# Batched matrix product on one core: outputs of two batches in one tile, stores of 6 KB rows, and another order of the rows of x in its loads

## The chip, the cores and the metric

The kernel runs on one core of one Trainium2 chip. The metric is the time of one execution in microseconds, as the device measures it. Before the change the median of nine runs is 136.33 us (lowest 136.18, highest 136.52).

## The reference

```python
batch, dim_i, dim_j, dim_k = 32, 256, 512, 384
x: (batch, dim_i, dim_j) float32
y: (batch, dim_j, dim_k) float32

def reference(x, y):
    return np.einsum('bij,bjk->bik', x, y).astype(np.float32)
```

There are 32 independent products of a 256 x 512 matrix by a 512 x 384 matrix. x is 16.8 MB, y 25.2 MB and the output 12.6 MB; each has to be moved once, 54.5 MB in all.

## The kernel before

The index j, over which the sum runs, has to lie in the partitions for the products. y comes so from memory (`load`, L69): partition q gets the four rows j = 4q to 4q + 3 of a batch, 6 KB in one run. x has j as its last index and has to be transposed on TensorE. It is loaded for four batches at once (Q = 4, L63), 2 MB, each partition taking 16 KB in one run: 32 partitions a batch, 8 rows of i in each.

`transpose(q)` (L71) makes 32 transposes of 128 x 128 for four batches, four to a PSUM bank `t_ps`. Each bank is then cast to fp16 into `xt_sb` by one copy, on DVE (L92) and ACT (L94) in turn; the copy writes with a step of four fp16 elements, so that a batch's 128 columns of i come to lie side by side. `round_y(b)` (L97) casts y of one batch to fp16 in four pieces, two on ACT (L102) and two on DVE (L104). `multiply(b)` (L106) makes eight products, each with 128 columns of x^T as weights and 384 columns of y streaming, into two banks `o_ps`, one for each half e of i. `collect(b)` (L124) copies the two banks to `o_sb`, one on ACT (L128) and one on DVE (L130). `store(b)` (L133) writes `o_sb` to memory, 3 KB in one run from each partition.

The order is written out by hand and kept (`keep`). The loop goes over the steps s = 0 to 33, and in each step issues, in this order: the loads of batch s + 6 (with x of four batches ahead of y where s + 6 is a multiple of four), the copies of batch s - 2, the products of batch s - 1, at every fourth step the transposes of four batches, the rounding of batch s, and the store of batch s - 2. Loads of the first six batches stand ahead of the loop.

All 72 DMAs, loads and stores, are issued by SP in this order, from one queue. In the compiled program they use eight completion counters in turn, and each DMA waits until the DMA eight places before it has finished; a store also waits for the copies on ACT and DVE, and a load of x for the transposes that free its buffer. Buffers: three for x, ten for y, four for rounded y, two for x^T, ten for `o_sb`; in PSUM four banks for `t_ps` and four for `o_ps`.

Of the kernel before, what the change touches and what calls it, by code (L numbers as in the profile page):

```python
# [1 line left out]

# [5 lines left out]


MM_DT = mybir.dt.float16  # L10
F32 = mybir.dt.float32
P = 128


Q = 4

LAG = 8

ON_ACT = ()


@with_exitstack
def kernel(
    ctx: ExitStack,
    tc: tile.TileContext,
    x: bass.AP,
    y: bass.AP,
    out: bass.AP,
):
    nc = tc.nc  # L30

    B, I, J = x.shape
    _, _, K = y.shape

    NI = I // P
    NJ = J // P


    R = Q * NI
    PQ = P // Q  # L40

    const_pool = ctx.enter_context(tc.tile_pool(name="const", bufs=1))
    x_pool = ctx.enter_context(tc.tile_pool(name="x_pool", bufs=3))
    y_pool = ctx.enter_context(tc.tile_pool(name="y_pool", bufs=10))
    yr_pool = ctx.enter_context(tc.tile_pool(name="yr_pool", bufs=4))
    xt_pool = ctx.enter_context(tc.tile_pool(name="xt_pool", bufs=2))
    o_pool = ctx.enter_context(tc.tile_pool(name="o_pool", bufs=10))
    tpsum_pool = ctx.enter_context(tc.tile_pool(name="tpsum", bufs=4, space=bass.MemoryType.PSUM))
    opsum_pool = ctx.enter_context(tc.tile_pool(name="opsum", bufs=4, space=bass.MemoryType.PSUM))


    keep = tc.keep_in_program_order

    identity = const_pool.tile([P, P], F32)
    make_identity(nc, identity)

    x_of, y_of, yr_of, xt_of, ps_of, o_of = {}, {}, {}, {}, {}, {}

    def load(b):
        if b % Q == 0:  # L60
            x_of[b // Q] = x_pool.tile([P, R, J], F32, name="x_sb")
            keep(
                nc.sync.dma_start(  # L63
                    out=x_of[b // Q],
                    in_=x[b : b + Q].rearrange("g (p r) j -> (g p) r j", r=R),
                )
            )
        y_of[b] = y_pool.tile([P, NJ, K], F32, name="y_sb")
        keep(nc.sync.dma_start(out=y_of[b], in_=y[b].rearrange("(q t) k -> q t k", q=P)))  # L69

    def transpose(q):  # L71

        x_sb = x_of.pop(q)
        xt_of[q] = xt_pool.tile([P, Q, NJ, NI, PQ, Q], MM_DT, name="xt_sb")
        n = 0
        for t in range(NJ):
            for e in range(NI):  # L80
                t_ps = tpsum_pool.tile([P, Q, Q, PQ], F32, name="t_ps")
                for h in range(Q):
                    keep(
                        nc.tensor.transpose(  # L84
                            t_ps[:, h].rearrange("c g p -> c (g p)"),
                            x_sb[:, h * NI + e, t::NJ],
                            identity,
                        )
                    )
                dst = xt_of[q][:, :, t, e].rearrange("c g p h -> c h g p")  # L90
                if n % 2 == 0:
                    keep(nc.vector.tensor_copy(dst, t_ps))  # L92
                else:
                    keep(nc.scalar.copy(dst, t_ps))  # L94
                n += 1

    def round_y(b):  # L97
        y_sb = y_of.pop(b)
        yr_of[b] = yr_pool.tile([P, NJ, K], MM_DT, name="y_r")
        for t in range(NJ):  # L100
            if t % 2 == 0:
                keep(nc.scalar.copy(yr_of[b][:, t], y_sb[:, t]))  # L102
            else:
                keep(nc.vector.tensor_copy(yr_of[b][:, t], y_sb[:, t]))  # L104

    def multiply(b):  # L106
        xt_sb, y_r = xt_of[b // Q][:, b % Q], yr_of.pop(b)
        ps_of[b] = [
            opsum_pool.tile([P, K], F32, name=f"o_ps_{e}", tag="o_ps")
            for e in range(NI)  # L110
        ]
        for t in range(NJ):
            for e in range(NI):
                keep(
                    nc.tensor.matmul(  # L115
                        ps_of[b][e],
                        xt_sb[:, t, e].rearrange("c p h -> c (p h)"),
                        y_r[:, t],
                        start=(t == 0),
                        stop=(t == NJ - 1),  # L120
                    )
                )

    def collect(b):  # L124
        o_of[b] = o_pool.tile([P, NI, K], F32, name="o_sb")
        for e in range(NI):
            if e % 2 == 0:
                keep(nc.scalar.copy(o_of[b][:, e], ps_of[b][e]))  # L128
            else:
                keep(nc.vector.tensor_copy(o_of[b][:, e], ps_of[b][e]))  # L130
        del ps_of[b]

    def store(b):  # L133
        eng = nc.scalar if b in ON_ACT else nc.sync
        keep(eng.dma_start(out=out[b].rearrange("(m e) k -> m e k", m=P), in_=o_of.pop(b)))  # L135


    ahead = LAG - 2
    for b in range(ahead):
        load(b)  # L140
    for s in range(B + 2):
        if s + ahead < B:
            load(s + ahead)
        if s >= 2:
            collect(s - 2)
        if 1 <= s <= B:
            multiply(s - 1)
        if s < B and s % Q == 0:
            transpose(s // Q)
        if s < B:  # L150
            round_y(s)
        if s >= 2:
            store(s - 2)


# [1 line left out]
_INS = ['x', 'y']  # L157
_OUTS = [((32, 256, 384), 'float32')]


# [23 lines left out]
```

## Time and profile before

| what | value |
|---|---|
| median of nine runs | 136.33 us |
| profiled execution, its own time | 136.32 us |
| its span, first to last instruction | 134.5 us |
| granted TensorE clock, mean | 0.904 |
| moved in the span | 54.62 MB, mean 406 GB/s |
| read from HBM / written to HBM | 41.94 MB / 12.58 MB |
| DMA packets | 10375, of which 1152 under 512 B |
| loads of y: number, size, issue to landing | 32, 768 KB, 15.1 us (median) |
| loads of x | 8, 2048 KB, 14.1 us |
| stores | 32, 384 KB, 14.1 us |
| first DMA issued | at 0.74 us |

The page divides the span into 40 slices and gives for each engine, and for the 16 DMA engines together, the busy share in tenths. A packet is one run of data as one DMA engine moves it: one 16 KB row of x, one 6 KB row of y, one 3 KB row of the output. The packets under 512 B carry no data; there are 16 for each of the 72 DMAs. "Issue to landing" is long because many DMAs stand in the queue at a time, so it tells of the queue, not of one transfer. The time of the profiled execution lies 1.8 us above its span.

### The profile page before, as it was taken

Reading aid. Unit: us, or ns where it says so; the run is one execution under the profiler, and the core shown is the slowest. Engines: PE = TensorE matmul, PEld = TensorE weight load, DVE = VectorE, ACT = ScalarE, POOL = GpSimd, SP = SyncE. Lnnn points to the kernel's source line nnn. Section 1 sums busy time; section 2 is a strip of 40 time slices with the busy share of each in tenths; the row PEclk is TensorE's granted clock in tenths of the full one; section 3 lists DMA queues with packets and bytes.
Section 4 is the critical chain, followed back from the end, with each engine's and each line's share of the span. In section 5 each row is a group of like instructions: output and inputs, shape, how many; then the busy total and the mean of one; then the engine's idle time right before and its main releaser. Section 6 shows DMA issues by size and latency. Waiting matters only on the chain.

```text
span 134.5 us, 1539 instructions
## 1 busy us (share of the span) xinstructions
PE 89.5 (67%) x512; PEld 65.5 (49%) x512; DVE 73.1 (54%) x128; ACT 79.8 (59%) x129; POOL 0.7 (1%) x6
## 2 busy tenths in 40 slices
PE   0039499949994938869195895949259492785900
PEld 0049346934693518735194454825159260783500
DVE  0007925893489614966079361977018870487610
ACT  3006965697579902996059860998009990289710
POOL 2000000000000000000000000000000000000000
PEclk9999959995999995999959589999968999689997
DMA  5999999999999999999999999999999999999992
GB/s 117 424 393 422 441 418 416 418 452 395 409 417 452 421 407 418 427 439 432 391 429 415 444 427 413 421 412 448 418 410 421 417 469 398 416 423 412 412 414 108
DMA packets 10375, 54.62 MB, mean 406 GB/s; under 512 B 1152, under 2 KB 1152, under 8 KB 9344
## 3 DMA queue, kind: packets, MB, share of 16 engines
q1 hardware_dynamic: 10368, 54.53, 98.1%
q8 instruction: 4, 0.07, 0.2%
q14 instruction: 3, 0.02, 0.0%
HBM read 41.94 MB, written 12.58 MB: 405 GB/s over the span
## 4 chain that ended last, share of the span: by engine, by line
DMA 90%; PE 1%; issue 1%; ACT 1%; SPq 1%; DVE 1%; DVEq 0%
DMA y_sb<-in_y_dram 47%; DMA out_dram<-o_sb 22%; DMA x_sb<-in_x_dram 21%; PE t_ps L84 1%; ACT y_r L102 1%; SPq L69 1%; DVE o_sb L130 0%; SPq L63 0%; DVE y_r L104 0%; ACT o_sb L128 0%; SPq L135 0%; DVEq L130 0%
## 5 line engine op out<-in xcount | busy, mean ns | idle before, releaser
L94 ACT CAST xt_sb<-t_ps 128x512 f16<-128x512 f32 x32 | 39.4, 1366 | 41.6 <-PE t_ps L84 41.5
L92 DVE CAST xt_sb<-t_ps 128x512 f16<-128x512 f32 x32 | 39.5, 1329 | 38.0 <-PE t_ps L84 38.0
L115 PE MATMUL o_ps<-y_r,xt_sb 128*128 128x384 f16 x256 | 48.1, 351 | 15.3 <-ACT y_r L102 15.3
L84 PE MATMUL t_ps<-identity,x_sb 128*128 128x128 f32 x256 | 41.8, 331 | 23.1 <-DMA x_sb<-in_x_dram 23.1
L84 PEld LDWEIGHTS t_ps<-identity,x_sb 128*128 128x128 f32 x256 | 39.5, 215 | 26.3 <-issue 24.9
L115 PEld LDWEIGHTS <-xt_sb 128*128 128x128 f16 x256 | 26.8, 105 | 35.7 <-issue 22.0
L102 ACT CAST y_r<-y_sb 128x384 f16<-128x384 f32 x64 | 30.1, 526 | 0.6 <-DMA y_sb<-in_y_dram 0.6
L130 DVE COPY o_sb<-o_ps 128x384 f32<-128x384 f32 x32 | 17.8, 555 | 17.0 <-PE o_ps L115 16.2
L104 DVE CAST y_r<-y_sb 128x384 f16<-128x384 f32 x64 | 19.8, 352 | 0.4 <-DMA y_sb<-in_y_dram 0.4
L128 ACT COPY o_sb<-o_ps 128x384 f32<-128x384 f32 x32 | 15.4, 483 | 5.6 <-PE o_ps L115 5.6
L94 ACT ACT_TABLE_LOAD x1 | 1.3, 1283 | 0.7 <-PEq L168 0.7
masks.py:199 POOL TENSOR_SCALAR_AFFINE_SELECT identity<-identity 128x128 f32<-128x128 f32 x1 | 0.3, 294 | 0.1
masks.py:197 POOL MEMSET identity<- 128x128 f32 x1 | 0.2, 205 | 0.3 <-POOLq L168 0.3
L168 POOL MEMSET const-bfloat16-1.0<- 128x1 bf16 x1 | 0.1, 102 | 0.0
L168 POOL MEMSET const-uint8-127<- 128x1 uint8 x1 | 0.1, 102 | 0.0
L168 POOL MEMSET const-float32-0.0<- 128x1 f32 x1 | 0.1, 99 | 0.2 <-issue 0.2
L168 POOL MEMSET const-float32-1.0<- 128x1 f32 x1 | 0.1, 99 | 0.0
## 6 DMA issues: line engine op xcount, KB each, us to landing
y_sb<-in_y_dram SPq DMA_DIRECT2D x32, 768.0 KB, 15.1
x_sb<-in_x_dram SPq DMA_DIRECT2D x8, 2048.0 KB, 14.1
out_dram<-o_sb SPq DMA_DIRECT2D x32, 384.0 KB, 14.1
```

The source lines that it names most:

```text
L69: keep(nc.sync.dma_start(out=y_of[b], in_=y[b].rearrange("(q t) k -> q t k", q=P)))
L84: nc.tensor.transpose(t_ps[:, h].rearrange("c g p -> c (g p)"), x_sb[:, h * NI + e, t::NJ], identity,)
L92: keep(nc.vector.tensor_copy(dst, t_ps))
L94: keep(nc.scalar.copy(dst, t_ps))
L102: keep(nc.scalar.copy(yr_of[b][:, t], y_sb[:, t]))
L104: keep(nc.vector.tensor_copy(yr_of[b][:, t], y_sb[:, t]))
L115: nc.tensor.matmul(ps_of[b][e], xt_sb[:, t, e].rearrange("c p h -> c (p h)"), y_r[:, t], start=(t == 0), stop=(t == NJ - 1),)
L128: keep(nc.scalar.copy(o_of[b][:, e], ps_of[b][e]))
L130: keep(nc.vector.tensor_copy(o_of[b][:, e], ps_of[b][e]))
L168: nc = _bacc.Bacc("TRN2", target_bir_lowering=False, num_devices=1)
```

## The change

G = 2 batches form a unit. For a unit, each product takes only 64 columns of x^T, and the two batches of the unit write into the lower and the upper 64 partitions of the same bank `o_ps`: a unit has four banks (e = 0 to 3) with eight products each. `collect` copies four full banks of a unit, and `store` writes two batches in one DMA, 6 KB in one run from each partition. y is still loaded batch by batch, 6 KB rows, two DMAs into one tile. The two halves of the transposes of four batches stand in two successive steps. Loads of x are issued one unit of y earlier. The loop runs over 16 units in 18 steps, with loads two units (four batches) ahead; buffers are halved in number where a buffer now holds two batches.

The load of x takes the same 128 pieces of 16 KB of four batches, but piece s = 16 v + w (v = 0 to 7, w = 0 to 15) goes to partition 8 w + v instead of partition s. The source of the DMA is written as 16 x 8 x 4096 elements (w, v, element), the destination as 128 partitions. The transposes put the columns back in order as they write to PSUM: the output is written with a step of 16 elements in runs of 8.

```diff
 Q = 4
-LAG = 8
+G = 2
+W = 16
+LAG = 4
...
-    NI = I // P
+    M = P // G
+    NE = I // M
     NJ = J // P
-    R = Q * NI
     PQ = P // Q
+    R = I // PQ
+    H = R // NE
+    U = B // G
...
-    y_pool = ctx.enter_context(tc.tile_pool(name="y_pool", bufs=10))
-    yr_pool = ctx.enter_context(tc.tile_pool(name="yr_pool", bufs=4))
+    y_pool = ctx.enter_context(tc.tile_pool(name="y_pool", bufs=5))
+    yr_pool = ctx.enter_context(tc.tile_pool(name="yr_pool", bufs=2))
...
-    o_pool = ctx.enter_context(tc.tile_pool(name="o_pool", bufs=10))
+    o_pool = ctx.enter_context(tc.tile_pool(name="o_pool", bufs=5))
...
-                    in_=x[b : b + Q].rearrange("g (p r) j -> (g p) r j", r=R),
+    def load_x(q):
+        x_of[q] = x_pool.tile([P, R, J], F32, name="x_sb")
+        keep(
+            nc.sync.dma_start(
+                out=x_of[q],
+                in_=x[q * Q : (q + 1) * Q]
+                .rearrange("g (p r) j -> (g p) (r j)", r=R)
+                .rearrange("(v w) s -> w v s", w=W),
+            )
+        )
+    def load(u):
+        if u == 0:
+            load_x(0)
+        if (u + 1) * G % Q == 0 and u + 1 < U:
+            load_x((u + 1) * G // Q)
+        y_of[u] = y_pool.tile([P, G, NJ, K], F32, name="y_sb")
+        for g in range(G):
+            keep(
+                nc.sync.dma_start(
+                    out=y_of[u][:, g],
+                    in_=y[u * G + g].rearrange("(q t) k -> q t k", q=P),
+                )
+            )
+    def transpose(q, half):
+        x_sb = x_of[q]
+        if half == 0:
+            xt_of[q] = xt_pool.tile([P, NJ, NE, Q * PQ, H], MM_DT, name="xt_sb")
+        n = 0
+        for t in range(half * NJ // 2, (half + 1) * NJ // 2):
+            for e in range(0, NE, 2):
+                t_ps = tpsum_pool.tile([P, 2, H, Q * PQ], F32, name="t_ps")
+                for f in range(2):
+                    for h in range(H):
+                        keep(
+                            nc.tensor.transpose(
+                                t_ps[:, f, h].rearrange("c (v w) -> c w v", w=W), x_sb[:, h * NE + e + f, t::NJ], identity
+                            )
+                        )
+                dst = xt_of[q][:, t, e : e + 2].rearrange("c f p h -> c f h p")
...
+    def multiply(u):
+        xt_sb, y_r = xt_of[u * G // Q], yr_of.pop(u)
+        ps_of[u] = []
+        for e in range(NE):
+            o_ps = opsum_pool.tile([P, K], F32, name="o_ps")
+            ps_of[u].append(o_ps)
+            for t in range(NJ):
+                for g in range(G):
+                    a = (u * G + g) % Q
+                    keep(
+                        nc.tensor.matmul(
+                            o_ps[g * M : (g + 1) * M],
+                            xt_sb[:, t, e, a * PQ : (a + 1) * PQ].rearrange("c p h -> c (p h)"),
+                            y_r[:, g, t],
+                            start=(t == 0),
+                            stop=(t == NJ - 1),
+                        )
+                    )
...
+    def store(u):
+        keep(
+            nc.sync.dma_start(
+                out=out[u * G : (u + 1) * G].rearrange("g (m e) k -> (g m) e k", e=NE),
+                in_=o_of.pop(u),
+            )
+        )
     ahead = LAG - 2
-    for b in range(ahead):
-        load(b)
-    for s in range(B + 2):
-        if s + ahead < B:
+    for u in range(ahead):
+        load(u)
+    for s in range(U + 2):
+        if s + ahead < U:
             load(s + ahead)
+        if s == 0:
+            transpose(0, 0)
+            transpose(0, 1)
         if s >= 2:
             collect(s - 2)
-        if 1 <= s <= B:
+        if 1 <= s <= U:
             multiply(s - 1)
-        if s < B and s % Q == 0:
-            transpose(s // Q)
-        if s < B:
+        if s < U:
             round_y(s)
+        for half in range(2):
+            q = (s + 1 - half) * G // Q
+            if (s + 1 - half) * G % Q == 0 and 0 < q < B // Q:
+                transpose(q, half)
         if s >= 2:
             store(s - 2)
```

`round_y` and `collect` keep their copies, with an index for the batch or the bank added.

## The prediction

> **What bounds the kernel now.** I read the page first: the slices of part 2, the queue of part 3 and the chain of part 4.
>
> ```profile
> PE 89.5 (67%) x512; PEld 65.5 (49%) x512; DVE 73.1 (54%) x128; ACT 79.8 (59%) x129; POOL 0.7 (1%) x6
> ...
> DMA  5999999999999999999999999999999999999992
> ...
> q1 hardware_dynamic: 10368, 54.53, 98.1%
> ...
> DMA 90%; PE 1%; issue 1%; ACT 1%; SPq 1%; DVE 1%; DVEq 0%
> ```
>
> The reader is to see that the 16 DMA engines are never idle between the first slice and the last, that their packets fill 98.1% of the span (0.981 x 134.5 = 131.9 us), and that no other engine passes 67%. So the kernel is bound by what its transfers cost, row by row, and a change counts as far as it changes that sum, or opens a hole in it.
>
> Next I asked what one row costs, in three stretches in which one kind of transfer runs alone: 4 to 7 us (x), 9 to 12 us (y) and 125 to 130 us (stores).
>
> ```profile
> DMA packets 76, 1.25 MB, mean 415 GB/s; under 512 B 0, under 2 KB 0, under 8 KB 0
> q1 hardware_dynamic: 76, 1.25, 97.7%
> ```
>
> ```profile
> DMA packets 240, 1.28 MB, mean 426 GB/s; under 512 B 32, under 2 KB 32, under 8 KB 240
> q1 hardware_dynamic: 240, 1.28, 102.0%
> ```
>
> ```profile
> DMA packets 757, 2.07 MB, mean 414 GB/s; under 512 B 84, under 2 KB 84, under 8 KB 757
> q1 hardware_dynamic: 757, 2.07, 103.0%
> ```
>
> Share times 16 engines times length, over the rows (packets under 512 B left out: they carry no data): x 0.977 x 48 / 76 = 0.617 us for a 16 KB row; y 1.02 x 48 / 208 = 0.2354 us for 6 KB; stores 1.03 x 80 / 673 = 0.1224 us for 3 KB. Check: 1024 x 0.617 + 4096 x 0.2354 + 4096 x 0.1224 = 2097 us over 16 engines = 131.1 us, against 131.9.
>
> Last the compute side, from the groups and from stretches of pure work at full clock (16 transposes, then 32 products):
>
> ```profile
> L94 ACT CAST xt_sb<-t_ps 128x512 f16<-128x512 f32 x32 | 39.4, 1366 | 41.6 <-PE t_ps L84 41.5
> L92 DVE CAST xt_sb<-t_ps 128x512 f16<-128x512 f32 x32 | 39.5, 1329 | 38.0 <-PE t_ps L84 38.0
> ...
> L102 ACT CAST y_r<-y_sb 128x384 f16<-128x384 f32 x64 | 30.1, 526 | 0.6 <-DMA y_sb<-in_y_dram 0.6
> L130 DVE COPY o_sb<-o_ps 128x384 f32<-128x384 f32 x32 | 17.8, 555 | 17.0 <-PE o_ps L115 16.2
> ```
>
> ```profile
> core 0: us, PE busy (x) PEld busy (x) DVE busy (x) ACT busy (x) POOL busy (x), PEclk, DMA share, GB/s
> 83.02:84.90 1.88, 1.88 (x16) 1.88 (x16) 1.19 (x2) 0.71 (x1) 0.00 (x0) 1.00 1.03 425
> 58.45:63.60 5.15, 5.15 (x32) 3.02 (x31) 3.12 (x9) 4.41 (x11) 0.00 (x0) 1.00 1.05 439
> ```
>
> The weight loads (3.02 us) lie inside the 5.15 us of the products: 161 ns a product. Transposes are 118 ns each at full clock and, in the stretch 51 to 53 us at clock 0.50, ten in 2.00 us. Compute waits for data most of the time; this is the cover that the change draws on.
>
> [...] a 16 KB row in 0.617 us is 26.6 GB/s on each engine, all 16 at once. [...]
>
> **The change part by part.**
>
> *Stores.* 32 stores of 3 KB rows become 16 of 6 KB rows. 4096 x 0.1224 = 501 us of engine time goes; 2048 rows of 6 KB come, priced like a y row, 2048 x 0.2354 = 482 us. (501 - 482) / 16 = 1.2 us less. That a 6 KB write costs what a 6 KB read does is bounded by the 3 KB rows: at worst twice 0.1224, which is no gain. I take -1.2.
>
> *Loads of x.* The bytes and the rows are the same. [...] a row takes about twice 0.617 us. Sum: 1024 x 0.617 / 16 = 39.5 us becomes 78; the fixed part of a row and of the slow first rows isn't doubled, so I take +38. Bounds: the least is -1, a gain at the start (between 1.8 and 8.8 us the queue moved 364 GB/s, at 420 that is 0.9 us shorter; elsewhere an x row is as quick per byte as a y row, 0.0386 us per KB against 0.0392, so there is nothing to gain in reading); the most is +40. I take the upper, since the engines have no slack: what a row costs more is paid in full.
>
> *Products.* 256 of 128 columns become 512 of 64 columns, in pairs that fill two halves of one bank. For two batches (a unit, 16 in all) that is 32 products. Overlapped in pairs: 16 x 161 ns = 2.6 us; one after another: 5.15 us. I take overlap[...]. Per unit the compute now forms one chain, because the four banks of a unit are all there are: products 2.6, 16 transposes 1.9, the last cast 1.3, the first copy 0.56 = 6.4 us, against (131.9 - 1.2) / 16 = 8.2 us of transfers, or 10.5 with slow x. Hidden; not hidden when the products don't overlap (8.9 us).
>
> *Transposes and casts.* The transposes now write PSUM in runs of single elements 64 B apart; bound 0 to 1.9 us a unit (twice as slow); I take 0. Casts keep count and size (64 of 512), with a destination step of 4 B instead of 8 B: between 1.35 us and half of it. Both lie under the transfers.
>
> *Order, buffers, waits.* SP issues load(s+2) ahead of store(s-2), both in units, so four loads of a unit stand between y(u)'s landing and store(u), as far ahead as before. A store waiting for its copies holds the loads behind it on SP; with up to eight DMAs in flight (each waits for the eighth before it) some 16 us of transfers are queued by then, against a collect about 14 us after its y landed (8.2 of the next unit's transfers, 2.0 of rounding, 2.6 of two casts, 1.0 of copies). One bank is now read by a copy that serves two batches: same copies, 64. No hole.
>
> *The end.* Stores 11 to 15 are left when the last y row has landed: four of them, 4 x 128 x 0.2354 / 16 = 7.5 us, lie ahead of the last. Its own chain: rounding 1, products 2.6 to 5.2[...], copy 0.6, issue and start about 1.5 = 5.7 to 8.3 us. 0 to 0.8 exposed; I take 0.3. The old end had none: nine stores were issued from 115.0 to 128.9 us and the engines worked on to the last slice.
>
> Sum against the profiled execution: 134.5 - 1.2 + 38 + 0.3 = 171.6 us of span; with the 1.8 us that its time (136.32) lies above the span, 173.4. The median of the runs is 136.33, so nothing is to be shifted; I say 173.
>
> **The rivals.**
>
> B, [...] only the stores count, 136.3 - 1.2 + 0.3 = 135.4 us, down to 134.6 if the start gains. [...] It is faster than before.
>
> C, [...] compute becomes the bound: column tiles don't overlap, chain of 8.9 us a unit. From the landing of the first unit (about 12.5 us) 16 x 8.9 = 142, plus the start, less what shorter casts give: about 152, 145 to 165. Its point of decision is 8.2 us a unit, that is 4.4 us for 32 products (137 ns each). For it: each product needs its weights loaded, and two loads now stand for each one before.
>
> D, [...] half the penalty, +19, is 155, from 142 to 163. [...]
>
> E, small holes only at the end or in the middle, 1 to 5 us: 136.6 to 141.
>
> **How the numbers follow.** Chances: A (the forecast[...]) 0.66; B 0.13, of which 0.02 within 0.2%; C 0.08; D 0.08; E 0.05. 0.2% (0.27 us) is what a measurement can tell here: nine runs lay from 136.18 to 136.52. A alone ranges from 164 (a penalty of four fifths) to 181 (full penalty, and 5 to 8 us lost at the end when products don't overlap). The range has to reach to D and most of C to leave out 0.2: 142 to 181. Faster 0.11, same 0.02, slower 0.87.
>
> **What would show it.** Right: in stretches where x rows run alone the queue moves about 210 GB/s where it moved 415, x packets take near 1.2 us, x from issue to landing far above 14.1 us, y and stores keep 415 to 430 GB/s, PE's share falls. Stores of 6 KB at 0.235 us show the first part. Wrong: x stretches at 415 GB/s (B, C); holes in the DMA slices (C, E); products of a pair that start 160 ns apart instead of together (C).

## The result, and the profile after

| what | before | after |
|---|---|---|
| median, runs on the same chip | 136.32 us (30 runs, 136.15 to 136.54) | 176.09 us (10 runs, 175.34 to 176.83) |
| ratio, 95% interval | | 1.2916 [1.29, 1.2931] |
| span of the profiled execution | 134.5 us | 175.1 us |
| granted TensorE clock, mean | 0.904 | 0.831 |
| mean rate in the span | 406 GB/s | 312 GB/s |
| duration of a 16 KB row of x, mean of 1024 | 0.627 us | 1.191 us |
| duration of a 6 KB row of y, mean of 4096 | 0.235 us | 0.248 us (with the stores' 6 KB rows, 6144) |

The changed kernel is slower by 29%. One execution of a variant below (the one with W = 32) took 179.85 us, with 32 products lasting 5.63 us where 2.79 us is their time at full clock, although its trace lists a granted clock of 1.0: its profile is not used, and a second profile of the same kernel stands for it.

The page of the changed kernel, parts 1 to 4: busy engines, slices, the queue and the chain of waits.

```profile
PE 101.8 (58%) x768; PEld 82.8 (47%) x768; DVE 56.3 (32%) x128; ACT 63.8 (36%) x129; POOL 0.7 (0%) x6
...
DMA  5989999999999999999999999999999999999994
GB/s 124 236 193 406 195 196 402 406 195 198 379 423 300 195 292 418 432 243 221 317 414 440 214 195 339 424 420 213 201 365 425 383 217 202 390 424 427 420 402 204
...
q1 hardware_dynamic: 8064, 54.53, 98.2%
...
DMA 83%; PE 10%; ACT 3%; DVE 0%; issue 0%
DMA x_sb<-in_x_dram 44%; DMA y_sb<-in_y_dram 39%; PE o_ps L135 8%; ACT xt_sb L112 2%; PE t_ps L104 2%; ACT y_r L121 1%; ACT o_sb L148 0%; DVE o_sb L150 0%
```

The DMA slices look as before: the engines are never idle, and their packets fill 98.2% of the span. From the busy share alone one would say that nothing is wrong with them. The line of GB/s says otherwise: with every engine busy it goes up and down between about 195 and 425, eight times. There are eight loads of x. No hole opened; certain rows got dearer.

The DMA view of the changed kernel from 4 to 7 us, where x runs alone, shows which. (Packets, megabytes and rate; then the queue's share of 16 engines' time.)

```profile
DMA packets 36, 0.59 MB, mean 197 GB/s; under 512 B 0, under 2 KB 0, under 8 KB 0
q1 hardware_dynamic: 36, 0.59, 95.3%
```

In the same stretch of the kernel before there were 76 rows at 415 GB/s. Now 36 rows of the same size keep the engines 95.3% busy: 0.953 x 48 / 36 = 1.27 us a row, where it was 0.617. (The view counts a row where it starts, so 36 rows in 3 us are a coarse rate; 16 rows of 16 KB in 1.27 us are 206 GB/s.) The same view from 130 to 134 us, with y and stores and no row of x:

```profile
DMA packets 307, 1.69 MB, mean 422 GB/s; under 512 B 32, under 2 KB 32, under 8 KB 307
q1 hardware_dynamic: 307, 1.69, 101.4%
```

1.014 x 64 / 275 = 0.236 us for a 6 KB row, as before. So whatever happens, happens while x is loaded.

Last the compute side. The timeline of the changed kernel (start, length, engine, line, operation; in brackets the idle time before it and who ended it), around 122 us and around 160 us:

```profile
121.97 2.79 PE L135 MATMUL o_ps<-y_r,xt_sb 128*64 128x384 f16 x32 [0.86 <-ACT xt_sb L112]
```

```profile
160.85 2.19 PE L104 MATMUL t_ps<-identity,x_sb 128*128 128x128 f32 x16
163.90 5.39 PE L135 MATMUL o_ps<-y_r,xt_sb 128*64 128x384 f16 x64 [0.87 <-ACT xt_sb L112]
```

32 products of 64 columns take 2.79 us, and 64 take 5.39: the second 32 add 2.60 us, 81 ns each, where a product of 128 columns took 161. In the records the two products of a pair start within 31 ns of each other, and the pairs follow one another every 158 to 162 ns: the two column tiles of a bank do work at the same time. 16 transposes take 2.19 us from the start of the first to the end of the last, and after the first they start 120 ns apart. (The prediction's stretch of 1.88 us ended before its last transpose did; in it, too, they start 120 ns apart.) The groups (part 5), and the issues of part 6 with the time from issue to landing in the last column:

```profile
L135 PE MATMUL o_ps<-y_r,xt_sb 128*64 128x384 f16 x512 | 57.9, 391 | 26.1 <-ACT o_sb L148 18.4
...
L112 ACT CAST xt_sb<-t_ps 128x512 f16<-128x512 f32 x32 | 22.4, 731 | 32.4 <-PE t_ps L104 32.4
L110 DVE CAST xt_sb<-t_ps 128x512 f16<-128x512 f32 x32 | 22.5, 728 | 32.6 <-PE t_ps L104 32.6
...
y_sb<-in_y_dram SPq DMA_DIRECT2D x32, 768.0 KB, 23.3
x_sb<-in_x_dram SPq DMA_DIRECT2D x8, 2048.0 KB, 31.1
out_dram<-o_sb SPq DMA_DIRECT2D x16, 768.0 KB, 22.9
```

The casts into `xt_sb` are nearly twice as fast as before (1366 and 1329 ns), which takes 17 us of work each from ACT and DVE, and the time has not gained by it: ACT's casts of this line are 2% of the chain. The mean of 391 ns for a product is a mean over different granted clocks (the 32 products from 113.51 us on took 5.33 us at a clock of 0.50, those from 121.97 us on 2.79 us at 1.00), and it counts two that overlap twice; it is no price.

### The profile page after: what moved, and what is told of

Same layout as the page of the kernel before. It is cut to its first block, busy times and chain, and to the rows that moved or that the text cites. A ratio compares the mean times of both kernels' runs of the same rounds, so it can differ in the third digit from the quotient of the medians.

```text
span 175.1 us, 1968 instructions
## 1 busy us (share of the span) xinstructions
PE 101.8 (58%) x768; PEld 82.8 (47%) x768; DVE 56.3 (32%) x128; ACT 63.8 (36%) x129; POOL 0.7 (0%) x6
## 3 DMA queue, kind: packets, MB, share of 16 engines
q1 hardware_dynamic: 8064, 54.53, 98.2%
HBM read 41.94 MB, written 12.58 MB: 311 GB/s over the span
## 4 chain that ended last, share of the span: by engine, by line
DMA 83%; PE 10%; ACT 3%; DVE 0%; issue 0%
DMA x_sb<-in_x_dram 44%; DMA y_sb<-in_y_dram 39%; PE o_ps L135 8%; ACT xt_sb L112 2%; PE t_ps L104 2%; ACT y_r L121 1%; ACT o_sb L148 0%; DVE o_sb L150 0%
## 5 line engine op out<-in xcount | busy, mean ns | idle before, releaser
L135 PE MATMUL o_ps<-y_r,xt_sb 128*64 128x384 f16 x512 | 57.9, 391 | 26.1 <-ACT o_sb L148 18.4
L104 PE MATMUL t_ps<-identity,x_sb 128*128 128x128 f32 x256 | 44.4, 343 | 41.4 <-DMA x_sb<-in_x_dram 41.4
L104 PEld LDWEIGHTS t_ps<-identity,x_sb 128*128 128x128 f32 x256 | 40.8, 216 | 46.8 <-issue 46.8
L135 PEld LDWEIGHTS <-xt_sb 128*64 128x64 f16 x512 | 42.0, 130 | 39.4 <-issue 21.5
L121 ACT CAST y_r<-y_sb 128x384 f16<-128x384 f32 x64 | 29.5, 513 | 71.0 <-DMA y_sb<-in_y_dram 70.9
L112 ACT CAST xt_sb<-t_ps 128x512 f16<-128x512 f32 x32 | 22.4, 731 | 32.4 <-PE t_ps L104 32.4
L110 DVE CAST xt_sb<-t_ps 128x512 f16<-128x512 f32 x32 | 22.5, 728 | 32.6 <-PE t_ps L104 32.6
L150 DVE COPY o_sb<-o_ps 128x384 f32<-128x384 f32 x32 | 16.3, 544 | 2.1 <-PE o_ps L135 2.1
L148 ACT COPY o_sb<-o_ps 128x384 f32<-128x384 f32 x32 | 13.9, 493 | 1.3 <-PE o_ps L135 1.3
```

The source lines that it names most:

```text
L104: nc.tensor.transpose(t_ps[:, f, h].rearrange("c (v w) -> c w v", w=W), x_sb[:, h * NE + e + f, t::NJ], identity)
L121: keep(nc.scalar.copy(yr_of[u][:, g, t], y_sb[:, g, t]))
L135: nc.tensor.matmul(o_ps[g * M : (g + 1) * M], xt_sb[:, t, e, a * PQ : (a + 1) * PQ].rearrange("c p h -> c (p h)"), y_r[:, g, t], start=(t ...
L148: keep(nc.scalar.copy(o_of[u][:, e], ps_of[u][e]))
L150: keep(nc.vector.tensor_copy(o_of[u][:, e], ps_of[u][e]))
```

## The experiments

The theory, T: the change of the order in the load of x changes which partitions are written together, and a row takes about twice as long for it, with 16 neighbouring partitions together about four times as long. Both factors were the author's estimates; no trace of the kernel before shows them. Rivals: that it is memory read in another order; that it is the form of the source (three dimensions); that it is something in the rest of the change; that it is the number of pieces a load is cut into.

### 1. All of the change but the order of x

```diff
-                .rearrange("g (p r) j -> (g p) (r j)", r=R)
-                .rearrange("(v w) s -> w v s", w=W),
+                .rearrange("g (p r) j -> (g p) r j", r=R),
...
-                                t_ps[:, f, h].rearrange("c (v w) -> c w v", w=W), x_sb[...], identity
+                                t_ps[:, f, h], x_sb[...], identity
```

> The changed kernel with the rows of x loaded in their own order again (128 outermost on both sides) and the transposes written without a step; the rest of the change stays. [...] the whole loss is in the spread load, so this ends at 135.1 us (136.3 - 1.2 from the 6 KB stores), 134.8 to 136.0, x rows back at about 0.62 us, y and store rows at 0.235 us. Rival (the column-tiled products, the halved number of buffers or the new order hold the transfers up): stays above 150 us.

Measured: 136.24 us (14 runs), ratio to the kernel before 0.9999 [0.9986, 1.0011]. From its page (slices, queue and chain):

```profile
DMA  5999999999999999999999999999999999999975
...
q1 hardware_dynamic: 8064, 54.53, 97.5%
...
DMA 78%; PE 13%; ACT 4%; DVE 0%; issue 0%
```

and its DMA view from 4 to 7 us:

```profile
DMA packets 77, 1.26 MB, mean 421 GB/s; under 512 B 0, under 2 KB 0, under 8 KB 0
q1 hardware_dynamic: 77, 1.26, 98.9%
```

x rows are back at 0.989 x 48 / 77 = 0.617 us, and the 40 us are gone. All of the loss lies in the order of x. What was left over: the gain of 1.2 us that the larger stores should have brought isn't there, and the time lies above the range that was expected. The last two slices of DMA are 7 and 5, where the kernel before had 9 and 2, so a hole at the end could have eaten it. Experiments 8 to 10 ask for that.

### 2. The order of x alone, on the kernel before

```diff
-                    in_=x[b : b + Q].rearrange("g (p r) j -> (g p) r j", r=R),
+                    in_=x[b : b + Q]
+                    .rearrange("g (p r) j -> (g p) (r j)", r=R)
+                    .rearrange("(v w) s -> w v s", w=16),
...
-                            t_ps[:, h].rearrange("c g p -> c (g p)"),
+                            t_ps[:, h].rearrange("c g p -> c (g p)").rearrange("c (v w) -> c w v", w=16),
```

> The kernel before with only the load of x spread over 16 x 8 and the transposes writing the columns back in order; products, stores and order as before. [...] +36 us from x rows of 1.19 us and +3 us from y rows beside them, so 173 to 177 us. Rival (the spread costs only together with the unit order, since x then stands beside y differently): under 150 us.

Measured: 176.7 us (4 runs), ratio 1.2988 [1.2951, 1.3025]. Rows of x take 1.174 us (mean of 1024). The page:

```profile
DMA packets 10375, 54.62 MB, mean 313 GB/s; under 512 B 1152, under 2 KB 1152, under 8 KB 9344
...
q1 hardware_dynamic: 10368, 54.53, 98.4%
```

As many packets as before the change, in a span of 174.4 us. The order of x is enough by itself, and with experiment 1 the rest of the change is ruled out. The difference of half a microsecond from the changed kernel (176.7 against 176.09) is no larger than the spread of each (176.2 to 177.53, and 175.34 to 176.83).

### 3 and 7. The same order with 32 pieces in place of 16

```diff
-W = 16
+W = 32
```

Piece s = 32 v + w goes to partition 4 w + v. The source still has three dimensions, memory is still read in steps (of 32 pieces in place of 16), and the transposes still write with a step.

> The changed kernel with W = 32 in place of 16: one number. The source is still of three dimensions with the pieces of x read in another order than they lie (piece 32 v + w), and the transposes still write with a step. [...] index w now covers only partitions 4w to 4w+3, [...] the time is that of the kernel with x in order, 134.8 to 136.0 us, x rows 0.62 us. [...] Rival (reading in another order than the memory's, or a source of three dimensions, is what is slow): 170 us or more as well, so only a fast run decides.

> The changed kernel with W = 32 once more, for a profile at the usual TensorE clock[...]. [...] span about 135.5 us, x rows near 0.62 us, stretches of x alone at about 415 GB/s; the 1.1 us that it lies above the kernel with x in order are to be found in the first DMA's start and in the end.

Measured: 137.39 us for experiment 3 (median of six runs), ratio 1.0078 [1.0063, 1.0092], and 137.17 for the run with the profile that is used here, whose page says:

```profile
DMA  4999999999999999999999999999999999999874
...
q1 hardware_dynamic: 8064, 54.53, 97.1%
...
x_sb<-in_x_dram SPq DMA_DIRECT2D x8, 2048.0 KB, 20.9
```

Rows of x take 0.622 us. One constant takes 39 us away. So the penalty comes neither from the three dimensions of the source, nor from the stepped writes of the transposes: both are still there. Memory is still read in another order than it lies, too, but not in the same other order, so that rival is left to experiments 5 and 6. The time lies above the range expected. The rest against the kernel before, 0.9 us, is in part the start (SP takes 0.64 us to issue the first load of x where it took 0.38, and the first packet moves at 2.19 us in place of 1.77), in part the end (8, 7, 4 in the last slices).

### 4, 5 and 6. The kernel before, its load of x cut into eight DMAs that write 128, 16 spaced or 16 neighbouring partitions

Here the rows of x stay in their natural order, and only the partitions that one DMA writes are chosen: 16 that lie 8 apart in experiment 5, 16 neighbours in experiment 6. The control (experiment 4) writes all 128 partitions in each of its eight DMAs, with rows of 2 KB.

```diff
-                    in_=x[b : b + Q].rearrange("g (p r) j -> (g p) r j", r=R),
+            rows = x[b : b + Q].rearrange("g (p r) j -> (g p) r j", r=R)
+            for v in range(8):
+                keep(nc.sync.dma_start(out=x_of[b // Q][:, v], in_=rows[:, v]))                                      # 4
+                keep(nc.sync.dma_start(out=x_of[b // Q][v::8], in_=rows[v::8]))                                      # 5
+                keep(nc.sync.dma_start(out=x_of[b // Q][16 * v : 16 * v + 16], in_=rows[16 * v : 16 * v + 16]))      # 6
```

(one of the last three lines in each kernel)

> The kernel before with each load of x issued as eight DMAs, each one 2 KB row (one r) into all 128 partitions: a control for the number of DMAs in the next two runs. An estimate from the rows: about 27 bytes per ns and 8 ns a row give 0.083 us for 2 KB, 64 x 8 rows an engine more dearly by 5.3 - 4.9 us a load of four batches, +3 us in all; with eight small DMAs in flight the queue is shorter, so 0 to 6 us on top: 138 to 146 us[...].

> The kernel before with each load of x issued as eight DMAs of 16 partitions, 8 apart (v, v+8, ... v+120), 16 KB rows, data in their own order: [...] every row of x in the partition where it was before. [...] rows take about 1.2 us as in the spread load, so 172 to 180 us. Rival (what costs is reading the rows of x in another order than before, neighbouring rows at once): engines here read rows 128 KB apart, so about the time of the control.

> The same with 16 neighbouring partitions in each of the eight DMAs (0 to 15, 16 to 31, ...): [...] a row takes about 2.45 us, x takes 64 x 2.45 = 157 us of each engine in place of 40, so about 250 us, 235 to 265. Rival (the number of DMAs or the order of reading): no slower than the run with partitions 8 apart[...].

One run each, beside one of the kernel before of 136.27 us:

| | time | row of x, mean (median) | of one row of 0.617 us |
|---|---|---|---|
| 4, eight DMAs, all partitions | 143.49 us | 0.089 us per 2 KB | 1.15, per byte |
| 5, partitions 8 apart | 176.05 us | 1.171 (1.251) us | 1.90 (2.03) |
| 6, 16 neighbours | 235.3 us | 2.028 (2.127) us | 3.29 (3.45) |

The page of experiment 5:

```profile
GB/s 128 233 199 419 352 233 188 417 361 229 188 398 425 369 199 223 407 420 331 226 228 417 422 315 218 262 418 415 289 218 292 424 440 220 213 353 411 421 412 203
...
q1 hardware_dynamic: 11264, 54.53, 98.9%
```

and of experiment 6:

```profile
GB/s 124 107 129 259 347 112 132 148 417 157 132 104 343 422 187 118 112 384 431 148 129 139 416 387 126 126 194 418 322 132 126 241 422 275 118 124 285 416 413 235
...
q1 hardware_dynamic: 11264, 54.53, 99.7%
```

Experiment 5 has nothing of the change in it, and yet its line of GB/s could be that of the changed kernel, and its time too (176.05 against 176.09); its median row, 1.251 us, is close to the changed kernel's 1.264. Experiment 6 reads memory in the most orderly way of all and is the slowest: slices that x alone fills stand between 104 and 132 GB/s, and 16 rows in 2.127 us are 123 GB/s. Eight DMAs a load, with rows of 2 KB, cost 7 us (experiment 4), against 40 and 99. Experiments 5 and 6 have the same number and size of DMAs. They differ in the set of partitions that one DMA writes, and with it in the rows of memory that are read together: 128 KB apart in experiment 5, neighbours in experiment 6. In these two runs both sides change together, so how much of the row time belongs to each was not separated, and no record says which rows the changed kernel moves at one moment. But the order of reading alone does not account for it: experiment 6 reads x in its natural order and has the dearest rows, while with W = 32 x is read in another order and rows take 0.622 us; and reading neighbours at once can't be the whole of it, since experiment 5 reads 128 KB apart and its rows take 1.90 times 0.617 us (2.03 by the median).

The dose was forecast as four times the row of before, 2.45 us, and about 250 us in experiment 6; it came to 2.03 and 235.3. The direction is T's, the size is not quite. The records show that the rows are not in step: in the first load, from about 5 us on, eight rows start some 0.7 us after the other eight, each lasting 2.2 us. Whether the missing part comes from this was not shown.

### 8, 9 and 10. The end of the kernel of experiment 1

Three steps, each on top of the one before. 8: the store of the last unit in two halves.

```diff
+        dst = out[u * G : (u + 1) * G].rearrange("g (m e) k -> (g m) e k", e=NE)
+        o_sb = o_of.pop(u)
+        if u < U - 1:
+            keep(nc.sync.dma_start(out=dst, in_=o_sb))
+        else:
+            for e in range(0, NE, 2):
+                keep(nc.sync.dma_start(out=dst[:, e : e + 2], in_=o_sb[:, e : e + 2]))
```

9: x one unit earlier. 10: the transposes one step earlier.

```diff
-        if (u + 1) * G % Q == 0 and u + 1 < U:
-            load_x((u + 1) * G // Q)
+        if (u + 2) * G % Q == 0 and u + 2 < U:
+            load_x((u + 2) * G // Q)
...
-            q = (s + 1 - half) * G // Q
-            if (s + 1 - half) * G % Q == 0 and 0 < q < B // Q:
+            q = (s + 2 - half) * G // Q
+            if (s + 2 - half) * G % Q == 0 and 0 < q < B // Q:
```

> The kernel with x in order (the change without the spread), and the store of the last unit in two DMAs of two banks each. Theory: x in order came out level with before because the end gives back what the 6 KB stores save: about 1.1 us of idle DMA engines between 124 and 133 us, while the last units are still being computed. Halving the last store lets its first half go about 1.3 us sooner: 0.3 to 0.6 us less, 135.6 to 136.0. Rival (the level result is the rows' own cost, not the end): 136.2, no change.

> The same, and each load of x one unit earlier, so that x of the last four batches lands before y of unit 12 rather than after it. Theory: the late chain of the end begins at the landing of that x (transposes, casts, copies, products), so it moves forward and the holes at the end shrink to under 0.3 us: 135.0 to 135.6. Rival (the end is held by the order on TensorE, not by x): as the run with the halved store alone.

> The same, and the two halves of the transposes one step earlier too, so that at the end no transposes stand between the products of units 13 and 14. Theory: TensorE is through sooner, no hole of over 0.2 us at the end, 134.9 to 135.4, faster than both kernels. Rival: transposes one step earlier wait for x on TensorE, with products of the step before behind them, and nothing is won over the run before.

Measured, 14 runs each, against 35 of the kernel before: 136.27 us, ratio 1.0 [0.9991, 1.001]; 136.3, 1.0001 [0.9992, 1.0009]; 136.18, 0.9993 [0.9982, 1.0004]. The page of experiment 10 (slices, then the chain):

```profile
DMA  5999999999999999999999999999999999999992
...
DMA 91%; PE 2%; DVE 1%; SPq 1%; issue 0%; DVEq 0%
```

The end is as tight as before the change (9 and 2), PE has all but gone from the chain (it had 13% in experiment 1), and the time has not moved. All three expectations missed, and what stood beside them as the rival held each time. Closing the hole won nothing that can be measured, so the hole had not eaten the gain. The DMA view of experiment 10 from 125 to 130 us, when the last y has landed and stores run alone (by the records all but 43 of their rows are of 6 KB), and one line of it from 126 to 129 us, where all are:

```profile
DMA packets 402, 2.07 MB, mean 415 GB/s; under 512 B 43, under 2 KB 43, under 8 KB 402
q1 hardware_dynamic: 402, 2.07, 100.2%
```

```profile
DMA packets 226, 1.25 MB, mean 418 GB/s; under 512 B 22, under 2 KB 22, under 8 KB 226
```

From 125 to 130 us the kernel before moved 757 packets, 673 of them 3 KB rows: 2.07 MB, 414 GB/s, 103.0%. About half as many rows bring the same bytes in the same time, within 1%. From 414 to 418 GB/s the 12.58 MB of the stores would gain 0.3 us, an estimate from these two rates, and such a gain would hardly show. The share above 100 means that rows of one engine overlap: by 3% for these 3 KB rows, by 2.0% for the 6 KB rows of y in the prediction. Added up, row times count the overlap twice. The bytes moved up to 100 us of the span say the same: 41.04 MB before, 41.04 in experiment 1, 41.07 in experiment 10 (summed from the packets' records).

## Why the prediction was right, and where not

The forecast was 173 us, with rows of x at about twice 0.617 us, and 176.09 was measured, inside the range and inside the likeliest case's own. The doubling, an estimate of the author's, held (1.264 us is the median row); the sum held by errors that partly cancel. From the durations of all packets in the two profiled executions:

| term | predicted | measured | how |
|---|---|---|---|
| loads of x | +38 us | +36.1 | 1024 / 16 x (1.191 - 0.627) |
| rows of y and of the stores | -1.2 | +3.8 | (6144 x 0.2476 - 4096 x 0.2351 - 4096 x 0.1213) / 16 |
| start | 0 | +0.4 | first packet at 2.19 us, was 1.77 |
| end and overlap of rows | +0.3 | +0.2 | what is left of 40.5 |
| span | 171.6 us | 175.1 | 134.55 + 40.5, by the records |

*Loads of x.* Right: 197 GB/s in the stretch (206 by the length of a row) where about 210 was to be seen, rows of 1.19 to 1.27 us against "near 1.2". Experiments 1 and 2 put the loss on this edit alone, 3 and 7 take away the form of the source and the stepped writes, and 5 and 6 bring the loss back in a kernel with no other part of the change, in an amount that goes with the set of rows that one DMA moves: 1.171 us a row for 16 partitions 8 apart, 2.028 for 16 neighbours. Why a row is dearer in such a set was not shown: no record says which engine moved a row, or which rows moved together in the changed kernel, and 5 and 6 change the partitions and the rows of memory together.

*Rows of y beside x.* This step failed in part. "y and stores keep 415 to 430 GB/s" holds from 130 to 134 us, where no x is moved (422, and 0.236 us a row), but over the whole the 6 KB rows rose from 0.235 to 0.248 us, one in a hundred to 0.47 or more. In experiment 2, where y and stores have rows of different size and so can be told apart, it is y alone: 0.252 us a row, with stores at 0.1216 against 0.1213. So loads of y pay for a load of x that runs beside them, about 4 us in all, and the prediction had nothing for it. Why it is y alone was not shown.

*Stores.* The term "I take -1.2" was mis-sized. It added up row times and took a shorter sum for a shorter transfer, and it priced a stored row like a row of y, though y alone ran at 426 GB/s and stores of 6 KB rows at 415 to 418. The bound that stood beside it, "at worst twice 0.1224, which is no gain", was near the answer: with rows of 3 KB the stores ran at 414 GB/s, and in experiments 1, 8, 9 and 10 the whole of the rest of the change is worth nothing that can be told from 0. The sign that was named for this part, 6 KB rows at 0.235 us, was seen (0.236), and the gain was not there all the same: the length of a row did not show it.

*Products, transposes, casts.* Overlap in pairs was right: from one unit to the next 2.60 us, as forecast. The stepped writes of the transposes cost 0, as taken. Experiment 1 writes without a step, and its 16 transposes, also 120 ns apart, take as long as the 2.19 us above:

```profile
109.68 2.16 PE L103 MATMUL t_ps<-identity,x_sb 128*128 128x128 f32 x16 [1.32 <-DMA x_sb<-in_x_dram]
```

The casts fell to the lower end of their bound. All of it lies under the transfers, so 34 us less work on ACT and DVE moved nothing. "Compute waits for data most of the time" said too much, with PE busy for 67% of the span; the cover was enough all the same.

*The end.* The 0.2 us that are left over hold the end and the overlap of rows together, so the 0.3 that was taken is not contradicted, and not shown either. In experiment 1 the last slices thinned out, but filling them in 8 to 10 won nothing measurable.

*The rivals.* B falls by the x rows (1.19 us). C falls by the pairs that overlap. D falls: the median row, 1.264 us, is 2.05 times 0.617, where half the penalty would make 1.5. E is not seen: after the start the DMA slices stay at 9, but for one 8, until the last. The lower end of A, 164 us, is a slip: with four fifths of the penalty its own sum gives 166.

No version tried is faster than the kernel before; the best, experiment 10, has a ratio whose interval includes 1.

## What to carry to other kernels

When DMA engines are all busy, read the rate beside the busy share: a line of GB/s that swings while the share stays at 9 (here between about 195 and 425) meant rows that had become dearer, and the duration of a row in a stretch where it runs alone said which (16 KB, 1.27 us in place of 0.617). When a load is rearranged, don't go by the partitions that it reaches by its end: here all 128 were reached in either case, and a row of x took 1.191 us in place of 0.627; the same rows in DMAs of 16 partitions took 1.171 and 2.028. And don't add up row times as if they were the cost of a transfer when the shares of the queue go above 100% (103.0% for the stores of 3 KB rows): here their sum promised 1.2 us, and the rate, 414 GB/s against 415 to 418, gave nothing that can be told from 0.

## What the runs showed of the hardware that was not expected

- Rows of 3 KB and of 6 KB are stored at the same rate within 1%, 414 and 415 to 418 GB/s; rows of 2 KB being loaded in eight DMAs cost 15% more per byte than one load of 16 KB rows (0.089 us each).
- In DMAs of 16 neighbouring partitions (experiment 6) a row of x took 3.29 times its 0.617 us (median 3.45) and not four times; in DMAs of 16 partitions 8 apart (experiment 5) 1.90 times (2.03).
- Casting from PSUM with a step of 4 bytes in the destination takes 731 and 728 ns (ACT and DVE), with a step of 8 bytes 1366 and 1329, for the same 128 x 512 elements. The runs at this step are also longer, 128 elements in place of 32; which of the two counts was not tested.
- SP needs 0.66 us to issue the load of x with its three-dimensional source for the first time, against 0.38 before.
- Stepping the PSUM writes of a transpose by 16 elements of 4 bytes costs nothing that shows: 16 of them take 2.19 us with the step and 2.16 without (experiment 1), 120 ns apart in both.
